# One transformer-like layer on one core: the branch projection's operands taken in groups, and the last product of the down projection added in banks that are already open

## The chip, the cores and the metric

The kernel runs on one core of a Trainium2 chip as a single launch. The metric is the device time of that launch in microseconds. A core has a matrix engine (TensorE, PE in the profile, with PEld for its weight loads), a vector engine (VectorE, DVE), a scalar engine (ScalarE, ACT), a general engine (GpSimd, POOL), a queue of DMA instructions on SyncE (SP, or SPq), the SBUF that all of them work in, and the PSUM, eight banks of 128 x 512 float32, in which TensorE adds its products up. Engines run at the same time, each through its own instructions in their order, and wait for one another on semaphores.

## What is computed

One layer on x, 1024 positions by 1024 columns. The lines of the reference that matter here:

```python
gates = jax.nn.sigmoid(zg.reshape(B_, S, N_BRANCH, D_MODEL) + b_gate)
merged = (gates[:, :, 0] * (ya @ w_branch[0])      # A: chunked attention
          + gates[:, :, 1] * (yb @ w_branch[1])    # B: forgetting attention
          + gates[:, :, 2] * (yc @ w_branch[2]))   # C: indexed sparse attention
return merged @ w_out
...
x = x + g1 * _rmsnorm(y, norm_g[l, 1])
h = _rmsnorm(x, norm_g[l, 2]) * (1.0 + sc2) + sh2
a, g = jnp.split(h @ w_up, 2, axis=-1)
y = (jax.nn.gelu(conv(a)) * g) @ w_down
x = x + g2 * _rmsnorm(y, norm_g[l, 3])
```

Each of ya, yb, yc is 1024 x 256, each w_branch 256 x 1024, w_down 2816 x 1024. The result must be close to float32, so a product of two matrices is taken as three: each operand is split into a high part (rounded to the engine's fast type) and a low part (what is left), and high x high, high x low and low x high are added.

## The kernel before

**Splitting.** `split` (L226 to L232 of the profile) makes the high part with one ACT copy (L231) and the low part with one DVE subtraction (L232).

**The attention heads and the branch stage.** The twelve heads are written by a hand-made order that mixes their score, transpose and value products with other work of TensorE, among it the gates (`g`, L247 to L249). The last head is the fourth of branch C: ACT and DVE make the high and low parts `C3ph` (L838) and `C3pl` (L839) of its transposed probabilities, and PE takes the products `C3y` (L822, L823). Where it is not ordered by hand, a scheduler places each engine's instructions. After the heads comes the branch stage: for each branch b (0 to 2) the two pieces `yb` of y are loaded from DRAM and split into `y_0h`, `y_0l`, `y_1h`, `y_1l`; then for each of eight column tiles m, the tile's weights (`wbr`, 128 x 2 x 128, 128 KB) are loaded (L1002), cast by ACT (L1003) and subtracted by DVE (L1004) into `wb`; the gate tile `tgb` comes back from DRAM (L1007; four gates of branch 2 are computed here instead); twelve matmuls `yp` (L1017 to L1019) fill two banks out of a ring of three; and DVE multiplies each bank by gate + 1 (L1021; into `M` for branch 0, into `tgb` after it). For branches 1 and 2 POOL adds that to `M` (L1023). `yb` and `tgb` share a ring of seven tiles (`k4`), `wbr` one of three.

**The down projection and the end.** The last part multiplies in rounds n = 0 to 6 with seven products per 2 x 2 block (a Strassen-like plan), each round into four banks; a table says which, and to which part of `acc` they are added. Round 4 uses the banks `V`, rounds 5 and 6 the banks `X`; `down_add` (L1643) adds a bank to `acc` on DVE. One inner slice of w_down is left over and taken as a plain product: its left operands are loaded from `F_spill` (into `ring`, L1513), its right ones are `wl`. `final_block` takes, for one block `tb` of 128 positions, that product in two halves of 512 columns (L1612 to L1614, six matmuls each, into banks of their own), and for each half: DVE adds the bank to `acc` (L1615), ACT squares it with a sum (L1616), POOL or DVE multiplies by the gain (L1617). Then DVE adds the two sums (L1619), DVE and POOL make the reciprocal root (L222, L224), DVE multiplies and adds the residual in two halves (L1623), and each half is stored. Even blocks go after round 4, odd blocks after round 6.

Of the kernel before, what the change touches and what calls it, by code (L numbers as in the profile page):

```python
# [27 lines left out]
N_RAW, N_E, N_K4, N_B4, N_STK, N_PT, N_BI, N_P4 = 3, 5, 7, 7, 4, 2, 1, 12  # L28
# [16 lines left out]
YG_POOL = (2, 2, 2, 2, 2, 2, 2, 1)  # L45
# [15 lines left out]
def encoder_layer(ctx: ExitStack, tc: tile.TileContext, x, w_ada, w_in, w_branch, w_out, w_up, w_down,  # L61
# [929 lines left out]

    M = [None] * KD
    for b in range(3):
        y_s = []
        for j in range(2):
            yt = k4(f"yb{b}_{j}")
            nc.sync.dma_start(yt, y_spill[b, j])
            y_s.append(split(yt, (P, S), f"y{b}_{j}", alloc=lambda n, sh: e4(n, sh, F32R)))
# [600 lines left out]
    def final_block(tb, banks):  # L1599
        xr = (e4 if tb % 3 else raw4)(f"xf{tb}")  # L1600
        nc.sync.dma_start(xr, x1_spill[tb * P:(tb + 1) * P, :])
        ss2 = sm(f"n3_{tb}ss2", 2)
        i, odd = tb // 2, tb % 2
        y, yg = acc[:, tb], work[:, 4 + i]
        sq = small.tile([P, HALF], F32, tag="ada_acc", name=f"sq{tb}", bufs=1)
        for e in range(2):
            o = banks[e]
# [1 line left out]
            for k in range(2):
                l, r = fin[k][0][odd], fin[k][1][e]  # L1610
                lh, ll = (l[:, j, i * P:(i + 1) * P] for j in range(2))
                pe.matmul(o, lh, r[:, 0], start=(k == 0), stop=False)  # L1612
                pe.matmul(o, lh, r[:, 1], start=False, stop=False)
                pe.matmul(o, ll, r[:, 0], start=False, stop=(k == 1))  # L1614
# [157 lines left out]
```

## Time and profile before

| | us |
|---|---|
| runs of the kernel before | 1581.08, 1584.87, 1584.56; median 1584.56 |
| the profiled execution | 1577.21 |
| its span in the trace | 1575.4 |
| PE busy | 1493.3 (95%) |
| DVE busy | 1157.1 (73%) |
| ACT busy | 787.0 (50%) |
| POOL busy | 559.6 (36%) |
| chain that ended last | PE 69%, DVE 15%, DMA 5%, issue 4%, ACT 4%, SPq 2%, POOL 1% |

The span is measured from the first instruction to the last in the trace; 1.8 us of the execution lie outside it. Busy shares are means over a span with very different stages, so they say which engine is full, and not where it waits: that is read from the timeline of PE, stretch by stretch. A bracket behind a row of a timeline is the time that the engine sat idle before that row, and the instruction that ended it.

### The profile page before, as it was taken

To read this page: it belongs to the slowest core of one execution; us is meant where nothing else is said; L and a number is where in the kernel's file an instruction comes from. 1 tells how busy PE (TensorE), PEld (TensorE's weight loads), DVE (VectorE), ACT (ScalarE), POOL (GpSimd) and SP (SyncE) were. 2 spreads that over 40 slices of the span, in tenths; PEclk is the share of its full clock that TensorE was granted. 3 is DMA by queue.
4 is the path that set the end of the run, shared out by engine and by line. 5 is a ranking of instruction groups with operands and counts; after the bars stand their busy time and mean duration, and the time that the engine had idled before them with its cause. 6 is when DMAs were issued, how large, how long until landed. Compare 5 with 4: busy or idle time off the path is not lost.

```text
span 1575.4 us, 21143 instructions
## 1 busy us (share of the span) xinstructions
PE 1493.3 (95%) x7322; PEld 1234.4 (78%) x7322; DVE 1157.1 (73%) x2106; ACT 787.0 (50%) x1462; POOL 559.6 (36%) x396
## 2 busy tenths in 40 slices
PE   3989999999998999998999989999999999999996
PEld 2878888887887788776888778788888887788885
DVE  6665888998559755557536779888778777879868
ACT  4434698886554444532235455555555554522222
POOL 3632544343443443205542323222223222323305
PEclk9999999999999999999999999999999999999999
DMA  9541332344443452346666412444444445898762
GB/s 287 137 107 47 105 111 84 124 129 131 122 132 90 121 160 88 111 150 204 217 265 215 142 54 94 170 158 166 152 146 164 153 148 173 329 354 293 280 227 108
DMA packets 181727, 253.98 MB, mean 161 GB/s; under 512 B 14891, under 2 KB 132851, under 8 KB 181619
## 3 DMA queue, kind: packets, MB, share of 16 engines
q1 hardware_dynamic: 181619, 252.62, 48.3%
q8 instruction: 58, 0.95, 0.3%
q14 instruction: 50, 0.41, 0.1%
HBM read 169.75 MB, written 74.97 MB: 155 GB/s over the span
## 4 chain that ended last, share of the span: by engine, by line
PE 69%; DVE 15%; DMA 5%; issue 4%; ACT 4%; SPq 2%; POOL 1%; DVEq 0%; POOLq 0%; ACTq 0%
PE g L247 4%; PE g L248 4%; PE X L1268 4%; PE g L249 4%; PE X L1269 4%; PE X L1270 4%; PE X L1632 2%; PE X L1633 2%; PE X L1634 2%; PE V L1268 2%; PE V L1269 2%; PE V L1270 2%; PE V L1632 2%; PE V L1633 2%; PE V L1634 2%
## 5 line engine op out<-in xcount | busy, mean ns | idle before, releaser
L669 ACT ACTIVATE junk<-sc,thr 128x512 bf16<-128x512 f32 (+2 forms) x93 | 80.1, 861 | 25.6 <-DVE thr L690 19.7
L671 DVE TENSOR_SCALAR_CACHE_REDUCE junk<-sc,thr 128x384 bf16<-128x384 f32 (+2 forms) x93 | 89.8, 966 | 1.9
L1234 POOL TENSOR_TENSOR T<-ua 128x512 f32<-128x512 f32 x21 | 27.2, 1294 | 175.7 <-DVE rT L1220 166.1
L1312 POOL TENSOR_TENSOR cv<-cv,g 128x1024 f32<-128x1024 f32 x22 | 57.1, 2598 | 49.3 <-ACT cv L1311 35.4
L1269 PE MATMUL X<-left_S,rT 128*128 128x512 f32 (+1 forms) x184 | 70.8, 385 | 0.2 <-DVE left_S L1114 0.2
L1268 PE MATMUL X<-left_S,rT 128*128 128x512 f32 (+1 forms) x184 | 70.8, 385 | 0.0
L1270 PE MATMUL X<-left_S,rT 128*128 128x512 f32 (+1 forms) x184 | 70.7, 384 | 0.0
L1522 ACT ACTIVATE T<-work 128x512 fp32r<-128x512 f32 x40 | 25.0, 631 | 63.2 <-PE V L1634 26.1
L1235 POOL TENSOR_TENSOR ug<-ug 128x512 f32<-128x512 f32 x22 | 33.0, 1501 | 65.2 <-DVE ua L1228 65.2
L1643 DVE TENSOR_TENSOR acc<-acc,X 128x512 f32<-128x512 f32 x68 | 45.7, 683 | 13.6 <-PE X L1634 13.3
L1023 POOL TENSOR_TENSOR M<-M,tgb 128x1024 f32<-128x1024 f32 x12 | 30.6, 2567 | 66.0 <-DVE tgb L1021 62.2
L585 DVE SCALAR_TENSOR_TENSOR ada_acc<-ada_row,c_act,ada_acc 128x512 f32<-128x512 f32 x42 | 39.3, 936 | 12.9 <-DMA ada_row<-in_w_ada 12.4
L1633 PE MATMUL X<-T,ring 128*128 128x512 f32 x120 | 47.0, 392 | 0.0
L1634 PE MATMUL X<-T,ring 128*128 128x512 f32 x120 | 46.7, 390 | 0.0
L1632 PE MATMUL X<-T,ring 128*128 128x512 f32 x120 | 46.2, 393 | 0.0
L1643 DVE TENSOR_TENSOR acc<-acc,V 128x512 f32<-128x512 f32 x56 | 37.3, 682 | 11.6 <-PE V L1634 11.1
L1220 DVE TENSOR_TENSOR rT<-ua,rT 128x512 fp32r<-128x512 f32 x45 | 38.7, 861 | 9.3 <-ACT rT L1219 9.0
L1219 ACT ACTIVATE rT<-ua 128x512 fp32r<-128x512 f32 x45 | 28.2, 627 | 33.0 <-DVE ua L1232 22.6
L1220 DVE TENSOR_TENSOR rB<-ua,rB 128x512 fp32r<-128x512 f32 x44 | 40.8, 931 | 2.0 <-ACT rB L1219 0.9
L1269 PEld LDWEIGHTS X<-left_S,rT 128*128 128x128 f32 x184 | 34.5, 187 | 8.0 <-DVE left_S L1114 0.4
L1270 PEld LDWEIGHTS X<-left_S,rT 128*128 128x128 f32 x184 | 34.5, 187 | 7.7
L637 DVE SCALAR_TENSOR_TENSOR sc<-rl,wi,sc 128x512 f32<-128x512 f32 (+3 forms) x30 | 30.2, 1038 | 14.0 <-ACT rl L636 14.0
(988 smaller groups left out, 5559.8 us busy)
## 6 DMA issues: line engine op xcount, KB each, us to landing
ring<-L_spill SPq DMA_DIRECT2D x70, 512.0 KB, 6.0
L_spill<-S SPq DMA_DIRECT2D x40, 512.0 KB, 4.0
L_spill<-A SPq DMA_DIRECT2D x30, 512.0 KB, 3.1
raw_g<-in_w_in SPq DMA_DIRECT2D x24, 512.0 KB, 4.1
ada_row<-in_w_ada SPq DMA_DIRECT2D x24, 512.0 KB, 4.0
ua<-in_w_up SPq DMA_DIRECT2D x22, 512.0 KB, 4.3
ug<-in_w_up SPq DMA_DIRECT2D x22, 512.0 KB, 3.9
gate_spill<-tg SPq DMA_DIRECT2D x20, 512.0 KB, 2.7
```

The costliest lines, as they stand in the source:

```text
L247: pe.matmul(o, wh[:, k], hh[:, k, ts_], start=(k == 0), stop=False)
L248: pe.matmul(o, wh[:, k], hl[:, k, ts_], start=False, stop=False)
L669: act.activation(junk_a[:, 0:n], scores[b], AF.Sign, scale=-1.0, bias=t_f, accum_out=cnt[:, j:j + 1])
L671: dve.tensor_scalar(junk_d[:, 0:n], scores[b], t_f, None, op0=OP.is_lt, op1=OP.add, accum_out=cnt[:, j:j + 1])
L1220: eng.tensor_tensor(hl_[1], src, hl_[0].bitcast(F32), op=OP.subtract)
L1268: pe.matmul(oc, r[:, 0, k], lh, start=(first and k == 0), stop=False, skip_group_check=True)
L1269: pe.matmul(oc, r[:, 0, k], ll, start=False, stop=False, skip_group_check=True)
L1270: pe.matmul(oc, r[:, 1, k], lh, start=False, stop=(last and k == 3), skip_group_check=True)
L1632: pe.matmul(o, lh, r[:, 0], start=(starts and k == 0), stop=False, skip_group_check=True)
L1633: pe.matmul(o, lh, r[:, 1], start=False, stop=False, skip_group_check=True)
L1634: pe.matmul(o, ll, r[:, 0], start=False, stop=(k == 1), skip_group_check=True)
L1643: dve.tensor_tensor(dst, dst, banks[i], op=OP.add)
```

## The change

Two places are changed.

**The branch stage.** The weights come in six loads of 512 KB, four column tiles each (`branch_w`), are split by `split` (one ACT copy, one DVE subtraction of 128 x 1024), and group g + 1 is asked for when tile 1 of group g is reached. The pieces of y are loaded and split by `branch_y`: those of branch 0 ahead of the stage, those of branch b + 1 loaded at tile 2 of branch b and split at tiles 4 and 6. The tiles of the low parts and the weights lie in other pools (the four slots `w4` of the gates' weights, thirteen slots `p4` where there were twelve).

**The end.** `final_block` becomes a class `Final` with four steps. In the last chunk, the half of the plain product that belongs to round 4's part of `acc` (columns 512 to 1023 of the even blocks) is added by PE in the bank `V` that still holds round 4's product, so one DVE addition takes both; so is the half that belongs to round 6's part (columns 0 to 511 of the odd blocks) in the bank `X`. The other halves have a bank of their own, as before. Eight DVE additions are gone (28 to 20 from round 4 on). The odd blocks are taken one by one within round 6, with ACT, DVE and POOL in written order.

```diff
-N_RAW, N_E, N_K4, N_B4, N_STK, N_PT, N_BI, N_P4 = 3, 5, 7, 7, 4, 2, 1, 12
+N_RAW, N_E, N_K4, N_B4, N_STK, N_PT, N_BI, N_P4 = 3, 5, 7, 7, 4, 2, 1, 13
...
+    def branch_y(b):
+        raws = []
+        for j in range(2):
+            raws.append(k4(f"yb{b}_{j}"))
+            nc.sync.dma_start(raws[j], y_spill[b, j])
+        n_y = iter(range(4))
+        def place(n, sh):
+            i = next(n_y)
+            return p4r(n, sh) if b == 1 and i else e4(n, sh, F32R)
+        def steps():
+            for j in range(2):
+                y_next.append(split(raws[j], (P, S), f"y{b}_{j}", alloc=place))
+                yield
+        return steps()
+    def branch_w(g):
+        rb = raw4(f"wbr{g}", (P, 2, HALF))
+        nc.sync.dma_start(rb, w_branch[g // 2][:, g % 2 * HALF:(g % 2 + 1) * HALF].rearrange("(k p) c -> p k c", p=P))
+        return split(rb, (P, 2, HALF), f"wb{g}", alloc=w4 if g < 4 else p4r)
...
     for b in range(3):
-        y_s = []
-        for j in range(2):
-            yt = k4(f"yb{b}_{j}")
-            nc.sync.dma_start(yt, y_spill[b, j])
-            y_s.append(split(yt, (P, S), f"y{b}_{j}", alloc=lambda n, sh: e4(n, sh, F32R)))
+        y_s, y_next = y_next, []
         for m in range(KD):
-            wb = p4r(f"wb{b}_{m}", (P, 2, 2, P))
-            rb = raw4(f"wbr{b}_{m}", (P, 2, P))
-            nc.sync.dma_start(rb, w_branch[b][:, m * P:(m + 1) * P].rearrange("(k p) c -> p k c", p=P))
-            act.activation(wb[:, 0], rb, AF.Copy)
-            dve.tensor_tensor(wb[:, 1], rb, wb[:, 0].bitcast(F32), op=OP.subtract)
+            if m % 4 == 0:
+                wb = wb_next
+            elif m % 4 == 1 and (b < 2 or m < 4):
+                wb_next = branch_w(b * 2 + m // 4 + 1)
+            if b < 2:
+                if m == 2:
+                    y_steps = branch_y(b + 1)
+                elif m in (4, 6):
+                    next(y_steps)
...
+                if c == N_C - 1 and n == 4:
+                    final_operands()
+                    evens = [Final(2 * i) for i in range(4)]
+                elif c == N_C - 1 and n == 6:
+                    odds = [Final(2 * i + 1) for i in range(4)]
+                    loads.enter_context(tc.manual_schedule(engines={E.Activation, E.DVE, E.Pool}))
                 for i, _ in enumerate(down_mm(n, next_ops())):
-                    down_add(n, i)
+                    if c < N_C - 1 or n not in (4, 6):
+                        down_add(n, i)
+                    elif n == 4:
+                        evens[i].half(1, VB[i], False)
+                        evens[i].gained(1)
+                    else:
+                        odds[i].half(0, XB[i], False)
+                        if i:
+                            odds[i - 1].norm()
+                        odds[i].gained(0)
+                        odds[i].half(1, VB[i], True)
+                        if i == 3:
+                            odds[3].gained(1)
+                            odds[3].norm()
+                        if i:
+                            odds[i - 1].end()
+                        if i < 3:
+                            odds[i].gained(1)
```

In the order of each engine, nothing is moved outside these two places. PE has the same matmuls in both kernels; DVE has 26 instructions fewer, ACT ten, SP eighteen.

On ACT, in head C3 (`C3e` are exponentials of its scores, `tg_4` a gate, `C3ph` the high parts that PE waits for), the kernel before has:

```order
L794 ACTIVATE C3e_6823,C3rs_6857<-C3e_6823,C3m_6838 128x640
L838 ACTIVATE C3ph_0_6873<-C3t_0_6868 128x512
L794 ACTIVATE C3e_6840,C3rs_6859<-C3e_6840,C3m_6855 128x768
L530 ACTIVATE tg_4_6768<-g_4_1_6782,gate_b 128x512
L838 ACTIVATE C3ph_1_6890<-C3t_1_6886 128x384
L846 ACTIVATE y_6004<-C3y_6867 64x256
L231 ACTIVATE y_0h<-yb_0_7091 128x1024
```

and the changed one:

```order
L793 ACTIVATE C3e_6823,C3rs_6857<-C3e_6823,C3m_6838 128x640
L837 ACTIVATE C3ph_0_6873<-C3t_0_6868 128x512
L793 ACTIVATE C3e_6840,C3rs_6859<-C3e_6840,C3m_6855 128x768
L230 ACTIVATE wb0h<-wbr_7103 128x1024
L529 ACTIVATE tg_4_6768<-g_4_1_6782,gate_b 128x512
L837 ACTIVATE C3ph_1_6890<-C3t_1_6886 128x384
L845 ACTIVATE y_6004<-C3y_6867 64x256
L230 ACTIVATE y_0h<-yb_0_7091 128x1024
```

The copy of the first weight group stands ahead of a gate and of `C3ph_1`. On DVE, the subtraction `wb0l` stands in the same way ahead of `C3pl_1`.

On PE, at the end of the last head (`C3t` transposes, `C3y` value products), the kernel before has:

```order
L833 MATMUL C3t_3_7063<-ident,C3e_6924 128x128 x2
L822 MATMUL C3y_7010<-C3ph_2_7047,Cv 128x256
L823 MATMUL C3y_7010<-C3pl_2_7048,Cv 64x256
L822 MATMUL C3y_7010<-C3ph_2_7047,Cv 128x256
L823 MATMUL C3y_7010<-C3pl_2_7048,Cv 64x256
L822 MATMUL C3y_7010<-C3ph_3_7067,Cv 128x256
L823 MATMUL C3y_7010<-C3pl_3_7068,Cv 64x256
L822 MATMUL C3y_7010<-C3ph_3_7067,Cv 128x128
L823 MATMUL C3y_7010<-C3pl_3_7068,Cv 64x128
L1017 MATMUL yp_0_0_7111<-y_0h,wb_0_7103 128x512
L1018 MATMUL yp_0_0_7111<-y_0l,wb_0_7103 128x512
```

and the changed one:

```order
L821 MATMUL C3y_7010<-C3ph_2_7047,Cv 128x256
L822 MATMUL C3y_7010<-C3pl_2_7048,Cv 64x256
L821 MATMUL C3y_7010<-C3ph_2_7047,Cv 128x256
L822 MATMUL C3y_7010<-C3pl_2_7048,Cv 64x256
L1046 MATMUL yp_0_0_7112<-y_1l,wb0h 128x512
L1047 MATMUL yp_0_0_7112<-y_1h,wb0l 128x512
L1046 MATMUL yp_0_1_7120<-y_1l,wb0h 128x512
L1047 MATMUL yp_0_1_7120<-y_1h,wb0l 128x512
L821 MATMUL C3y_7010<-C3ph_3_7067,Cv 128x256
L1046 MATMUL yp_1_0_7137<-y_1l,wb0h 128x512
L1047 MATMUL yp_1_0_7137<-y_1h,wb0l 128x512
L822 MATMUL C3y_7010<-C3pl_3_7068,Cv 64x256
```

Eighteen `yp` matmuls (twelve of them further up, between the transposes and `C3y_2`) stand among the head's own products, where all of them came behind it. Further on, on DVE, the subtraction of the first y piece of branch 2 stands ahead of branch 1's first multiplication, and those of weight group 3 and of the second piece behind that one and the next.

On DVE at the end (`acc` additions, `n_5ss` to `n_7` the steps to a block's factor, `xf` the last multiplication and addition), the kernel before ends with:

```order
L1615 TENSOR_TENSOR acc<-acc,X_12167 128x512
L1617 TENSOR_TENSOR work<-acc,G_1_12173 128x512
L1623 SCALAR_TENSOR_TENSOR xf_13912<-work,n_3r,xf_13912 128x512 x2
L1619 TENSOR_TENSOR n_7ss<-n_7ss_13978 128x1
L1623 SCALAR_TENSOR_TENSOR xf_13944<-work,n_5r,xf_13944 128x512 x2
L222 TENSOR_SCALAR n_7_14000<-n_7ss 128x1
L1623 SCALAR_TENSOR_TENSOR xf_13976<-work,n_7r,xf_13976 128x512 x2
```

and the changed one with:

```order
L1647 TENSOR_TENSOR acc<-acc,V_12086 128x512
L1665 SCALAR_TENSOR_TENSOR xf_13771<-work,n_3r,xf_13771 128x512 x2
L1647 TENSOR_TENSOR acc<-acc,X_12083 128x512
L1658 TENSOR_TENSOR n_5ss<-n_5ss_13776 128x1
L221 TENSOR_SCALAR n_5_13897<-n_5ss 128x1
L1647 TENSOR_TENSOR acc<-acc,V_12087 128x512
L1654 TENSOR_TENSOR work<-acc,G_1_12089 128x512
L1658 TENSOR_TENSOR n_7ss<-n_7ss_13779 128x1
L221 TENSOR_SCALAR n_7_13914<-n_7ss 128x1
L1665 SCALAR_TENSOR_TENSOR xf_13774<-work,n_5r,xf_13774 128x512 x2
L1665 SCALAR_TENSOR_TENSOR xf_13777<-work,n_7r,xf_13777 128x512 x2
```

Each odd block's last step now stands right behind the next block's second addition, where three blocks' last steps stood in a row at the end.

## Rows read from the trace of the kernel before

**Rows 1.** Stretches: from:to, length, busy us (count) by engine, granted clock, DMA share, GB/s

```profile
720.00:740.00 20.00, 17.10 (x74) 13.38 (x73) 14.08 (x18) 3.55 (x8) 13.21 (x6) 1.00 0.73 233
...
760.00:780.00 20.00, 20.00 (x90) 16.50 (x89) 9.36 (x11) 5.79 (x9) 8.58 (x4) 1.00 0.72 258
...
691.00:695.00 4.00, 3.91 (x10) 3.08 (x11) 1.25 (x3) 1.14 (x4) 0.00 (x0) 0.57 0.74 267
```

**Rows 2.** Timeline of PE, head C3: start, duration, operation, idle before and releaser

```profile
670.41 0.33 PE L823 MATMUL C3y<-C3pl,Cv 128*64 128x256 f32 x1 [0.20 <-DVE C3pl L839]
...
681.40 0.38 PE L822 MATMUL C3y<-C3ph,Cv 128*128 128x256 f32 x1 [0.41 <-ACT C3ph L838]
681.99 0.33 PE L823 MATMUL C3y<-C3pl,Cv 128*64 128x256 f32 x1 [0.21 <-DVE C3pl L839]
...
690.13 0.33 PE L823 MATMUL C3y<-C3pl,Cv 128*64 128x256 f32 x1 [0.66 <-DVE C3pl L839]
...
691.09 0.51 PE L1017 MATMUL yp<-y_0h,wb 128*128 128x512 f32 x1 [0.51 <-ACT wb L1003]
```

**Rows 3.** Timeline of PE, branch stage: its rows with idle time, one neighbour

```profile
703.55 0.40 PE L1019 MATMUL yp<-y_1h,wb 128*128 128x512 f32 x1
705.30 0.51 PE L1017 MATMUL yp<-y_0h,wb 128*128 128x512 f32 x1 [1.36 <-ACT wb L1003]
...
718.72 0.73 PE L1017 MATMUL yp<-y_1h,wb 128*128 128x512 f32 x2 [0.74 <-ACT y_1h L231]
723.59 0.50 PE L1017 MATMUL yp<-y_0h,wb 128*128 128x512 f32 x1 [1.83 <-DVE tgb L1021]
738.67 0.50 PE L1017 MATMUL yp<-y_0h,wb 128*128 128x512 f32 x1 [1.07 <-DVE tgb L1021]
745.20 0.50 PE L1017 MATMUL yp<-y_0h,wb 128*128 128x512 f32 x1 [0.65 <-DVE tgb L1021]
```

**Rows 4.** Waits from 680 to 757: us in total, times, longest

```profile
ACT y_0h L231 <- DMA yb<-y_spill: 12.1, 2, 7.8
ACT wb L1003 <- DMA wbr<-in_w_branch: 11.7, 5, 3.6
```

**Rows 5.** Timeline of ACT, head C3: a copy of 128 x 1024

```profile
671.30 1.06 ACT L231 ACTIVATE y_0h<-yb 128x1024 fp32r<-128x1024 f32 x1
```

**Rows 6.** Timeline of DVE, head C3 and start of branch 1: three subtractions

```profile
679.80 1.22 DVE L232 TENSOR_TENSOR y_0l<-yb,y_0h 128x1024 fp32r<-128x1024 f32 x1
...
722.51 0.43 DVE L1004 TENSOR_TENSOR wb<-wbr,wb 128x256 fp32r<-128x256 f32 x1 [2.58 <-ACT wb L1003]
...
724.64 2.32 DVE L1004 TENSOR_TENSOR wb<-wbr,wb 128x256 fp32r<-128x256 f32 x1
```

**Rows 7.** Tile tgb: shortest, median and longest time of its loads

```profile
DMA to landing us min/median/max: 3.4/4.5/7.8
```

**Rows 8.** Timeline of POOL at the end: root of block 2, two gain products

```profile
1542.95 0.55 POOL L224 TENSOR_TENSOR n_2r<-n,mhalf 128x1 f32<-128x1 f32 x1
1543.47 3.00 POOL L1617 TENSOR_TENSOR work<-acc,G 128x512 f32<-128x512 f32 x2
```

**Rows 9.** Timeline of DVE at the end: block 2's last step, an addition, the last row

```profile
1543.53 3.48 DVE L1623 SCALAR_TENSOR_TENSOR xf<-work,n_2r,xf 128x512 f32<-128x512 f32 x2 [0.16 <-POOL n_2r L224]
...
1547.00 0.67 DVE L1615 TENSOR_TENSOR acc<-acc,V 128x512 f32<-128x512 f32 x1
...
1570.81 1.41 DVE L1623 SCALAR_TENSOR_TENSOR xf<-work,n_7r,xf 128x512 f32<-128x512 f32 x2 [0.66 <-POOL n_7r L224]
```

**Rows 10.** Timeline of PE at the end: first plain product, last matmul

```profile
1531.58 0.39 PE L1612 MATMUL V<-wl,ring 128*128 128x512 f32 x1
...
1563.17 0.40 PE L1614 MATMUL X<-wl,ring 128*128 128x512 f32 x1
```

**Rows 11.** Timeline of SP: stretch in which the four F_spill loads are issued

```profile
1514.90 7.81 SPq L1513 DMA_DIRECT2D ring<-F_spill  x4
```

**Rows 12.** Tile ring from 1512 on: shortest, median and longest time of its loads

```profile
DMA to landing us min/median/max: 3.5/5.9/6.6
```

More of the change, by code (lines that the diff above doesn't have):

```diff
@@ L44 @@
 L_AHEAD = 4
-YG_POOL = (2, 2, 2, 2, 2, 2, 2, 1)
 N_BANKS = {"d": 2, "s": 3, "n": 3}
@@ L1597, in final_operands @@
                                                None if j else w4) for e in range(2)]))
[L1599 to L1607, printed above, removed]
-            es = slice(e * HALF, (e + 1) * HALF)
[L1609 to L1614, printed above, removed]
-            dve.tensor_tensor(y[:, es], y[:, es], o, op=OP.add)
-            act.activation(sq, y[:, es], AF.Square, accum_out=ss2[:, e:e + 1])
-            (pool if e < YG_POOL[tb] else dve).tensor_tensor(yg[:, es], y[:, es], G2[e], op=OP.mult)
-        ss = sm(f"n3_{tb}ss")
-        dve.tensor_tensor(ss, ss2[:, 0:1], ss2[:, 1:2], op=OP.add)
-        r = rstd_of(ss, f"n3_{tb}")
-        for e in range(2):
-            es = slice(e * HALF, (e + 1) * HALF)
-            dve.scalar_tensor_tensor(xr[:, es], yg[:, es], r, xr[:, es], op0=OP.mult, op1=OP.add)
-            nc.sync.dma_start(out[tb * P:(tb + 1) * P, es], xr[:, es])
@@ new lines, in encoder_layer, with __init__, half, gained @@
+    class Final:
+        def __init__(self, tb):
+            self.tb, self.i, self.odd = tb, tb // 2, tb % 2
+            self.xr = (e4 if tb % 3 else raw4)(f"xf{tb}")
+            nc.sync.dma_start(self.xr, x1_spill[tb * P:(tb + 1) * P, :])
+            self.ss2 = sm(f"n3_{tb}ss2", 2)
+            self.y, self.yg = acc[:, tb], work[:, 4 + self.i]
+        def half(self, e, o, start):
+            for k in range(2):
+                l, r = fin[k][0][self.odd], fin[k][1][e]
+                lh, ll = (l[:, j, self.i * P:(self.i + 1) * P] for j in range(2))
+                pe.matmul(o, lh, r[:, 0], start=(start and k == 0), stop=False, skip_group_check=True)
+                pe.matmul(o, lh, r[:, 1], start=False, stop=False, skip_group_check=True)
+                pe.matmul(o, ll, r[:, 0], start=False, stop=(k == 1), skip_group_check=True)
+            es = slice(e * HALF, (e + 1) * HALF)
+            y = self.y[:, es]
+            dve.tensor_tensor(y, y, o, op=OP.add)
+            sq = small.tile([P, HALF], F32, tag="ada_acc", name=f"sq{self.tb}", bufs=1)
+            act.activation(sq, y, AF.Square, accum_out=self.ss2[:, e:e + 1])
+        def gained(self, e):
+            es = slice(e * HALF, (e + 1) * HALF)
+            y = self.y[:, es]
+            (dve if e and self.tb == NB - 1 else pool).tensor_tensor(self.yg[:, es], y, G2[e], op=OP.mult)
+        def norm(self):
+            ss = sm(f"n3_{self.tb}ss")
+            dve.tensor_tensor(ss, self.ss2[:, 0:1], self.ss2[:, 1:2], op=OP.add)
+            self.r = rstd_of(ss, f"n3_{self.tb}")
+        def end(self, halves=(0, 1)):
+            tb, xr, r = self.tb, self.xr, self.r
+            for e in halves:
+                es = slice(e * HALF, (e + 1) * HALF)
+                dve.scalar_tensor_tensor(xr[:, es], self.yg[:, es], r, xr[:, es], op0=OP.mult, op1=OP.add)
+                nc.sync.dma_start(out[tb * P:(tb + 1) * P, es], xr[:, es])
```

28 lines of the change are left out of this document (17 added, 11 removed).

## The prediction

> **What bounds the kernel now.** The first view is the busy time by stretch [rows 1]. From 760 on PE is busy all the time (20.00 us of 20, 90 matmuls, so 0.22 us from one to the next); a change elsewhere can't shorten that. From 720 to 740 it is busy 17.10 us, and no other engine is full, so there something is waited for. Between 691 and 695 the granted clock is 0.57: most of that stretch ran at the lower of the clock's two levels (1.2 GHz), right behind the gaps at the end of head C3.
>
> The second view is the timeline of PE in those stretches, of which the rows with an idle bracket count. At the end of head C3 four stand from 681.40 on [rows 2]: 0.41, 0.21, 0.66 and 0.51 us, three ended by C3's own high and low parts, the last by the first weight cast. In the branch stage there are five [rows 3]: 1.36, 0.74, 1.83, 1.07, 0.65, sum 5.65. An idle gap costs more than its bracket: from 703.55 to 705.30 are 1.75 us where 0.23 is usual, that is 0.16 over the 1.36 of the bracket, and the matmul behind it lasts 0.51 instead of 0.40. So I add 0.28 for each gap.
>
> The third view says who was late. ACT waited 12.1 us for the two loads of y and 11.7 us in five waits for weights [rows 4]; since it works in order, the cast that PE needs stood behind them. Later PE waits for DVE's multiplication, which stands behind a weight subtraction: 0.43 us alone, 2.32 us for the same size once POOL adds to M [rows 6].
>
> At the end, PE is through at 1563.17 + 0.40 = 1563.57 and DVE at 1570.81 + 1.41 = 1572.22 [rows 9, 10]: 8.65 us in which the matrix engine does nothing.
>
> **The change part by part.**
>
> (1) End of head C3. Eighteen yp matmuls are put between the head's products. That is 18 x 0.22 = 4.0 us of work where the four gaps are, 1.79 us, with 0.28 each 2.9 us. Cover is lost for the last pieces only: weight group 1's subtraction (1.22 us, as long as the first row of [rows 6]) now stands ahead of the last C3pl on DVE, and the next yp waits for a bank that is emptied behind that. Two of the eighteen stand in this place, so I leave 0.5 us of stall. Gain 2.4 us, bounds 1 and 2.9.
>
> (2) The clock. 691 to 695 at 0.57 is 4.0 x 0.43 = 1.7 us lost. The low level came after PE had idled at 690 and 691 [rows 2]; with those gaps filled I expect full clock. Gain 1.7, bounds 0 (the same happens at another gap) and 1.7.
>
> (3) The first weight group in head C3. Its copy (1.06 us, [rows 5]) stands ahead of C3ph_1 on ACT, its subtraction (1.22 us) ahead of C3pl_1 on DVE. There PE already waited 0.20 us for C3pl_1 at 670.41 [rows 2], so there is no slack: C3pl_1 comes some 1.06 to 1.3 us later, and PE, whose next scores stand behind C3y, with it. I take a loss of 1.3; bounds 0.8 (part of it is made up by the scores' own waits behind it) and 2.5 (copy and subtraction one after the other, and the gap's 0.28).
>
> (4) The branch stage. The casts are ahead by four tiles and y by a branch, so the waits of [rows 4] need no longer end a gap of PE: the five gaps, 5.65 + 5 x 0.28 = 7.1 us, can go. 18 casts and 18 subtractions fewer cost nothing where they were and aren't on the path. What is late next: at the start of branch 1, DVE holds the subtraction of branch 2's first y piece ahead of the first multiplication, then weight group 3, then the second piece, three of 1.22 us. The load behind the first is issued on SP after a gate tile that waits until branch 1's own second piece is split, at tile 6 of branch 0; some six loads of 512 KB are then in flight at once, and such loads landed after 3.4 to 7.8 us, median 4.5 [rows 7]. Three banks give PE two groups of six matmuls, 2.7 us, before it waits for the first multiplication. With the median I get the multiplication late by 0.4 to 3 us beyond that and take 1.2; for weight group 5, whose subtraction meets POOL at work as in the last row of [rows 6], 0.5. So 7.1 - 1.7 = 5.4, bounds 2 and 7.1.
>
> (5) The F_spill loads are needed earlier: the first plain product was at 1531.58 [rows 10] and now stands 23 matmuls, 5.1 us, sooner, at about 1526.5. The four loads are issued from 1514.90 on within 7.81 us [rows 11] and landed after at most 6.6 us [rows 12], so the first pair is there at about 1522, and the third load, needed some 13 matmuls later, by 1529.3 at the worst. No cost; if that cover fails, PE waits one for one.
>
> (6) The end. Eight DVE additions of 0.67 us [rows 9] go, 5.4 us of work. Are they on the path? An odd block's last step takes 1.41 us alone and 3.48 us, in the last and the first row of [rows 9], when POOL has its two gain products (3.00 us, started 0.06 us earlier, [rows 8]): the two engines take turns. In the changed order each odd block has just this pattern, POOL's root (0.55), then its two gains against DVE's two halves (3.48), one further addition (0.67) and the small steps (about 0.3): 5.0 us for each block, while PE needs 18 x 0.22 = 4.0 us. So DVE and POOL set the pace, the removed additions shorten what DVE had waited for, and the last block's steps end about when they did. I take a gain of 0.3; bounds -1.3 (one more gain product of POOL in the last chain) and 5.4 (all of the additions). Of the two ends I stay near the lower one, because the row of 3.48 is the same pattern.
>
> The Trainium skill has a rule on that place, in "SBUF — State Buffer", section "Who interferes with whom": a DVE instruction with two SBUF inputs contends with a GpSimd instruction that reads SBUF, the one that issues first goes on and the other blocks, and one with at most one SBUF input doesn't contend. By that rule the additions from PSUM are the very DVE work that POOL doesn't hold up, so taking them out frees nothing of the held chain; the trace agrees (3.48 us against 1.41). By a count of DVE's instructions alone the sum would be 5.1 us better.
>
> **Sum.** 2.4 + 1.7 - 1.3 + 5.4 + 0.3 = 8.5 us. The profiled execution took 1577.21 us and would take 1568.7, its span 1566.9 instead of 1575.4. The median of the three runs shown is 1584.56, 7.35 us over the profiled one; taking the gain from it gives **1576.1 us**.
>
> **The rivals.**
>
> (a) The end gives all its additions back: DVE isn't held by POOL in the new order, and the tail after the last matmul shrinks from 8.65 to about 3.5 us. For it: the tail is long, and the odd blocks are spread out. Against: the 3.48 us. 1576.1 - 5.1 = 1571.0.
>
> (b) The branch stage's gaps come back as late gate tiles and y pieces: these share seven tiles, y now holds two of them for most of a branch, and a landing of 7.8 us instead of 4.5 delays every multiplication. For it: the last three gaps of [rows 3] are ended by the multiplication, not by a cast, and the DMA share there is 0.73 already [rows 1]. Then (4) brings nothing: 1576.1 + 5.4 = 1581.5.
>
> (c) The change doesn't do what it says at the end of C3: weight group 1 is copied into a slot of a gate's weights and so waits on ACT for the last of that gate's matmuls, with the head's last C3ph behind it; yp then fills no gap, and the clock still falls. (1) and (2) are lost: 1576.1 + 4.1 = 1580.2.
>
> (d) Slower: late 512 KB loads stop PE so long that the clock falls each time, as at 691. One such place costs 7.8 - 4.5 = 3.3 us of wait, 0.28, and 1.7 of clock, 5.3 us. The places are the start and middle of branch 1 and the start of branch 2, with (3) as a fourth that adds 1.7. All: 15.9 + 1.7 - 1.7 (the stalls that the sum already holds) = 15.9, so 1576.1 + 15.9 = 1592.0. From two places on the kernel is slower than before. Against it: DMA stands at 0.73, and the clock stayed at 1.00 through the gaps of 720 to 740 [rows 1].
>
> **How the numbers follow.** Forecast 0.55, (a) 0.13, (b) 0.17, (c) 0.10, (d) 0.05. The forecast's own range, with the bounds of (1) to (6), is 1572.5 to 1580. The range from 1570.5 to 1582 takes in (a), (b) and (c) and leaves (d) and the far ends out. A measurement of this kernel tells a difference from none at about 0.3%, 4.75 us: faster is below 1579.8, slower above 1589.3. Faster: nearly all of the forecast (0.53), (a) (0.13), a third of (c) and a fifth of (b) (0.07): 0.73. Slower: 0.04, from (d). Within: 0.23.
>
> **What would show it.** Right: no idle bracket on PE between 681 and 692, granted clock 1.00 there, one gap near 670 of about 1.3 us, at most 1.7 us of gaps between 692 and 745, and still over 8 us from the last matmul to DVE's last row, with pairs of 3.5 us in DVE's last multiplications. Wrong: gaps ended by a gate tile's load or by ACT's copies in branch 1 (b, d), a row of C3 ended by ACT behind the copy of weight group 1 (c), or a tail of 4 us (a).

## The result and the profile after

| | median, us | runs, us | ratio to before |
|---|---|---|---|
| before | 1583.85 | 1581.08 to 1584.87 (4) | |
| changed | 1573.33 | 1570.51 to 1576.28 (4) | 0.9938, 95% interval 0.9920 to 0.9956 |

In all that follows two runs are left out that fell in a slow state, one of 7479.96 us of the kernel before and one of 2919.52 us of `gain_one_half`.

The change makes the kernel faster, by 7 to 13 us on the interval. The profiled execution of the changed kernel took 1573.15 us, its span 1571.3. The two spans differ by only 4.1 us, because the profiled execution of before was a quick one: its projection banks `pm`, in code that both kernels share, begin at 78.91 us, and at 82.53 to 83.74 in the changed kernel and in all nine experiments. So the gain is read from one mark to another inside the trace, not from span to span. Three marks on PE serve for the whole study: the last row of the matmuls `ada_ps` in the heads, which comes ahead of both edits' effects, the 19th `yp` matmul, by which all of head C3 and the same eighteen `yp` matmuls are done in either order, and the first matmul `row` behind the branch stage. Timeline of PE, before (start, duration, engine, line, operation; in brackets the idle time before it and what ended it):

```profile
635.66 0.50 PE L588 MATMUL ada_ps<-one,ada_acc 128*128 128x1 f32 x4
...
696.91 0.39 PE L1018 MATMUL yp<-y_1l,wb 128*128 128x512 f32 x1
...
809.70 0.49 PE L1043 MATMUL row<-ident,mod 128*128 128x128 f32 x3
```

And of the changed kernel, with every row between the first and the last mark that has an idle bracket from 668 on:

```profile
639.07 0.51 PE L587 MATMUL ada_ps<-one,ada_acc 128*128 128x1 f32 x4
...
674.18 0.39 PE L821 MATMUL C3y<-C3ph,Cv 128*128 128x256 f32 x1 [0.67 <-ACT C3ph L837]
675.10 0.34 PE L822 MATMUL C3y<-C3pl,Cv 128*64 128x256 f32 x1 [0.53 <-DVE C3pl L838]
...
696.26 0.50 PE L1046 MATMUL yp<-y_1l,wb0h 128*128 128x512 f32 x1 [0.68 <-DVE y_1l L231]
...
699.10 0.50 PE L1045 MATMUL yp<-y_0h,wb0h 128*128 128x512 f32 x1 [0.78 <-DVE M L1049]
...
804.51 0.60 PE L1071 MATMUL row<-ident,mod 128*128 128x128 f32 x4
```

From the first mark to the last: 174.04 us before, 165.44 after, 8.6 us less. The gaps of [rows 2] and [rows 3] are gone, and four others stand in head C3. The row of 699.10 is the 19th `yp`: up to there it was 61.25 us before and 60.03 after, from there on 112.79 and 105.41. So 1.2 us of the gain lie ahead of that mark and 7.4 behind it. The windows (busy us and count of PE, PEld, DVE, ACT, POOL; granted clock, DMA share, GB/s) answer to [rows 1]:

```profile
691.00:695.00 4.00, 4.00 (x28) 3.60 (x27) 1.40 (x3) 2.07 (x3) 0.00 (x0) 1.00 0.00 0
...
700.00:720.00 20.00, 20.00 (x90) 16.51 (x89) 15.51 (x22) 5.92 (x6) 0.00 (x0) 1.00 0.97 348
720.00:740.00 20.00, 20.00 (x89) 16.37 (x88) 10.86 (x15) 1.06 (x1) 18.21 (x8) 1.00 0.62 201
```

PE is full from 700 on, with 90 and 89 matmuls in 20 us, where 74 stood from 720 to 740 in [rows 1]. The DMA share is 0.97 from 700 to 720, and no gap comes of it. ACT still waits long there, 12.7 us for a slot of weight group 5 and 7.7 for y, and in this execution PE is not late for that:

```profile
ACT wb5h L230 <- PE yp L1046: 12.7, 1, 12.7
...
ACT y_0h L230 <- DMA yb<-y_spill: 7.7, 1, 7.7
```

The y of that second wait is covered by little: its copy on ACT starts at 716.72 and takes 1.06 us, and DVE's subtraction of it, which stands ahead of branch 1's first multiplication, starts at 718.11, 0.33 us after the copy's end. Experiment 3 shows an execution in which that cover fails.

At the end the changed kernel has the pattern of the first row of [rows 9] twice. Timeline of DVE, of the odd blocks 1 and 3 and of the last, 7:

```profile
1551.33 0.69 DVE L1647 TENSOR_TENSOR acc<-acc,X 128x512 f32<-128x512 f32 x1 [0.75 <-PE X L1644]
1551.93 0.76 DVE L1658 TENSOR_TENSOR n_1ss<-n_1ss 128x1 f32<-128x1 f32 x1
...
1553.55 3.49 DVE L1665 SCALAR_TENSOR_TENSOR xf<-work,n_1r,xf 128x512 f32<-128x512 f32 x2
...
1557.55 0.14 DVE L1658 TENSOR_TENSOR n_3ss<-n_3ss 128x1 f32<-128x1 f32 x1
...
1558.55 3.44 DVE L1665 SCALAR_TENSOR_TENSOR xf<-work,n_3r,xf 128x512 f32<-128x512 f32 x2
...
1566.77 1.41 DVE L1665 SCALAR_TENSOR_TENSOR xf<-work,n_7r,xf 128x512 f32<-128x512 f32 x2
```

and of POOL and PE in the same place:

```profile
1550.13 2.55 POOL L1654 TENSOR_TENSOR work<-acc,G 128x512 f32<-128x512 f32 x2 [2.19 <-DVE acc L1647]
...
1553.48 3.01 POOL L1654 TENSOR_TENSOR work<-acc,G 128x512 f32<-128x512 f32 x2
...
1559.37 0.40 PE L1644 MATMUL V<-wl,ring 128*128 128x512 f32 x1
```

PE is through at 1559.77 and DVE at 1568.18: a tail of 8.41 us where [rows 9, 10] gave 8.65. From the mark `row` to the end of the last matmul are 753.87 us before and 755.26 after, 1.39 more. The other traces have 754.54 to 757.41 there, and the longest is `end_alone`, which has the stage of before; `branch_alone`, with the end of before, has 755.30. So I take this for a difference between executions; what makes it stays open.

### The profile page after: what moved, and what is told of

Its sections match the earlier page's. It is cut to its first block, busy times and chain, and to the rows that moved or that the text cites. A ratio compares the mean times of both kernels' runs of the same rounds, so it can differ in the third digit from the quotient of the medians.

```text
span 1571.3 us, 21017 instructions
## 1 busy us (share of the span) xinstructions
PE 1488.9 (95%) x7322; PEld 1231.8 (78%) x7322; DVE 1144.9 (73%) x2080; ACT 783.3 (50%) x1444; POOL 557.3 (35%) x396
## 4 chain that ended last, share of the span: by engine, by line
PE 69%; DVE 17%; DMA 4%; issue 4%; ACT 3%; SPq 2%; POOL 1%; DVEq 0%; ACTq 0%; POOLq 0%
PE X L1296 4%; PE X L1297 4%; PE X L1298 4%; PE g L246 4%; PE g L247 4%; PE g L248 4%; PE X L1674 2%; PE X L1675 2%; PE X L1676 2%; PE V L1296 2%; PE V L1297 2%; PE V L1298 2%; PE V L1674 2%; PE V L1675 2%; PE V L1676 2%
## 5 line engine op out<-in xcount | busy, mean ns | idle before, releaser
L584 DVE SCALAR_TENSOR_TENSOR ada_acc<-ada_row,c_act,ada_acc 128x512 f32<-128x512 f32 x42 | 39.3, 937 | 12.7 <-DMA ada_row<-in_w_ada 12.3
```

## The experiments

The theory (A): the stage brings nearly all, by gaps of PE that go; the end brings nothing, because DVE and POOL take turns there. The rivals are in the expectations: that the two edits share the gain, that one half of the stage's edit does it alone, that the end is held by something else.

**1. Each edit alone.** `branch_alone` is the changed kernel with the old `final_block`, `end_alone` the kernel before with the new end:

```diff
# branch_alone, against the changed kernel
-                    elif n == 4:
-                        evens[i].half(1, VB[i], False)
...
+                    for i in range(4):
+                        final_block(2 * i, VB[i % 2 * 2:i % 2 * 2 + 2])
...
```

> Only the branch stage is changed (weights in groups of four column tiles, y one branch ahead), the end is that of the kernel before. Theory A (the stage brings nearly all, the end's additions were off the path): about 8.6 us faster than before, ratio 0.9946, no idle bracket on PE in branches 1 and 2, tail from the last matmul to the last row of DVE 8.6 us as before. Rival B (both parts matter, the end brings 4 to 5 us that one profile hides): 4 to 5 us faster, ratio 0.997.

> Only the end is changed (the last plain product is added in the open banks, odd blocks one by one), the branch stage is that of the kernel before. Theory A: 0.2 to 0.3 us faster, ratio 1.000 within its interval, tail 8.4 us, pairs of 3.5 us in DVE's last multiplications of the odd blocks. Rival B: 4 to 5 us faster, ratio 0.997, tail about 4 us.

| | median, us | ratio to before | interval |
|---|---|---|---|
| branch_alone | 1572.51 | 0.9944 | 0.9928 to 0.9959 |
| end_alone | 1582.68 | 1.0002 | 0.9991 to 1.0014 |

The stage alone is the whole gain, as far as these runs can tell (8.9 us, 6.5 to 11.4, against the 9.8 of both edits), and the end alone moves nothing that they can tell. From mark to mark `branch_alone` takes 165.74 us. `end_alone` has the stage of before, in a second execution, and it shows which of the gaps of [rows 2, 3] are fixed and which are chance. Timeline of PE, `end_alone`:

```profile
686.10 0.39 PE L822 MATMUL C3y<-C3ph,Cv 128*128 128x256 f32 x1 [0.41 <-ACT C3ph L838]
686.69 0.33 PE L823 MATMUL C3y<-C3pl,Cv 128*64 128x256 f32 x1 [0.21 <-DVE C3pl L839]
...
694.83 0.33 PE L823 MATMUL C3y<-C3pl,Cv 128*64 128x256 f32 x1 [0.66 <-DVE C3pl L839]
...
695.79 0.50 PE L1017 MATMUL yp<-y_0h,wb 128*128 128x512 f32 x1 [0.51 <-ACT wb L1003]
...
710.70 0.50 PE L1017 MATMUL yp<-y_0h,wb 128*128 128x512 f32 x1 [3.65 <-ACT wb L1003]
```

The four gaps of C3 [rows 2] come back to the hundredth (0.41, 0.21, 0.66, 0.51). The clock behind them doesn't. A window of `end_alone`, which answers to 692 to 694 of before (its first `yp` starts at 695.79, that of before at 691.09):

```profile
696.00:698.00 2.00, 2.00 (x10) 1.62 (x10) 0.68 (x3) 0.86 (x3) 0.00 (x0) 1.00 0.72 250
```

and of before:

```profile
692.00:694.00 2.00, 2.00 (x6) 1.51 (x6) 0.00 (x0) 0.19 (x1) 0.00 (x0) 0.50 0.78 281
```

Ten matmuls in 2 us at full clock against six at 0.50. So the 1.7 us of half clock were lost in the one profile of before and not in the other execution of the same code. In `end_alone` the cast of the first gap of [rows 3] came later: ACT stood 8.57 us for the load of y ahead of it, and PE idled 3.65 us where before had 1.36.

**2. y ahead alone, weights in groups alone.** In `y_ahead` the weights come tile by tile as before; in `w_groups` y is loaded at the start of its own branch as before. Both keep the new end.

```diff
# y_ahead
-            if m % 4 == 0:
-                wb = wb_next
-            elif m % 4 == 1 and (b < 2 or m < 4):
-                wb_next = branch_w(b * 2 + m // 4 + 1)
+            wb = p4r(f"wb{b}_{m}", (P, 2, 2, P))
+            rb = raw4(f"wbr{b}_{m}", (P, 2, P))
...
+            act.activation(wb[:, 0], rb, AF.Copy)
+            dve.tensor_tensor(wb[:, 1], rb, wb[:, 0].bitcast(F32), op=OP.subtract)
...
# w_groups
-        y_s, y_next = y_next, []
+        y_s = []
+        for j in range(2):
+            yt = k4(f"yb{b}_{j}")
+            nc.sync.dma_start(yt, y_spill[b, j])
+            y_s.append(split(yt, (P, S), f"y{b}_{j}", alloc=lambda n, sh: e4(n, sh, F32R)))
...
```

> The changed kernel, except that the weights of the branch stage come tile by tile as before (128 KB, a cast and a subtraction for each tile); y is loaded and split one branch ahead. No yp matmul then stands among head C3's products. Theory A (the gaps of the branch stage have two causes, late weights and late y, and the end of C3 needs the weight groups): the gaps ended by y's copy go, those ended by weight casts and by multiplications behind weight subtractions partly stay; the end of C3 keeps its four gaps and its half clock. From the last ada_ps matmul to the first row matmul 169 to 171 us (before 173.8, after 165.2), ratio to before about 0.998. Theory B (ACT standing behind y's loads was the cause of all five gaps): 166.5 us, ratio 0.9955.

> The changed kernel, except that y is loaded and split at the start of its own branch as before; the weights come in groups of four tiles, one group ahead. The 18 yp matmuls stand among head C3's products as in the changed kernel. Theory A (y must be ahead as well): the end of C3 is as in the changed kernel, but at the starts of branches 1 and 2 PE stands 2 to 5 us for y's load, copy and subtraction, and the clock may fall: from the last ada_ps matmul to the first row matmul 170 to 175 us, ratio 0.997 to 1.001. Theory C (the groups alone bring it): 166 us, ratio 0.995.

All times from the first mark, in us (the expectations count from the last of the four `ada_ps` matmuls, 0.25 us later than the start of their row):

| | 19th yp | row | between | ratio to before |
|---|---|---|---|---|
| before | 61.25 | 174.04 | 112.79 | |
| end_alone (stage of before) | 59.64 | 173.69 | 114.05 | 1.0002 |
| changed | 60.03 | 165.44 | 105.41 | 0.9938 |
| branch_alone | 60.03 | 165.74 | 105.71 | 0.9944 |
| y_ahead | 59.66 | 167.89 | 108.23 | 0.9973, 0.9960 to 0.9985 |
| w_groups | 60.03 | 167.67 | 107.64 | 0.9957, 0.9943 to 0.9971 |

Neither theory of the expectations holds in full. I had given `y_ahead` 169 to 171 us or 166.5, and `w_groups` 170 to 175 or 166; both lie between. By the marks each half by itself takes about 6.1 to 6.4 us from the stage, and the two together 8.6: they remove the same waits to a large part. The times of the runs are too coarse for that: by their ratios `y_ahead` gains 4.3 us (2.4 to 6.3), `w_groups` 6.8 (4.6 to 9.0) and both 9.8 (7.0 to 12.7). Four gaps are left in `y_ahead` behind C3, none over 0.42 us, two ended by weights and two by multiplications; three of them are

```profile
705.93 0.50 PE L1046 MATMUL yp<-y_0h,wb 128*128 128x512 f32 x1 [0.42 <-DVE wb L1026]
...
717.62 0.50 PE L1046 MATMUL yp<-y_0h,wb 128*128 128x512 f32 x1 [0.41 <-DVE wb L1026]
...
743.20 0.47 PE L1044 MATMUL yp<-y_0h,wb 128*128 128x512 f32 x1 [0.28 <-DVE tgb L1048]
```

and `w_groups` has one behind its 19th `yp`:

```profile
723.97 0.50 PE L1044 MATMUL yp<-y_0h,wb2h 128*128 128x512 f32 x1 [1.22 <-DVE tgb L1048]
```

ACT's waits fit that. The waits of `y_ahead` from 680 to 757 (us in total, times, longest) have

```profile
ACT wb L1025 <- DMA wbr<-in_w_branch: 18.6, 6, 4.5
```

and those of `w_groups`

```profile
ACT y_0h L230 <- DMA yb<-y_spill: 4.4, 2, 2.8
```

In `y_ahead` ACT stood longer for weights than before (18.6 us against the 11.7 of [rows 4]), but for a load of y only 0.4 us, once, and PE lost little by it: a late cast no longer had a second late load in front of it. In `w_groups` ACT stood 4.4 us for y where before had 12.1. That the two waits covered each other in this way is how I read these rows; the runs themselves show only that the gains overlap.

The second column says what the eighteen `yp` matmuls between C3's products are worth. `y_ahead` has none of them there and all four old gaps, at full clock, and no weight group in head C3; it is 0.37 us sooner at the 19th `yp` than the changed kernel. A window of it, with the gaps of 0.66 and 0.51 us (ended at 692.35 and 693.31):

```profile
692.00:694.00 2.00, 1.14 (x6) 0.90 (x7) 0.98 (x3) 1.31 (x4) 0.00 (x0) 1.00 0.95 297
694.00:696.00 2.00, 2.00 (x11) 1.62 (x10) 0.69 (x2) 0.41 (x2) 0.00 (x0) 1.00 0.79 278
```

So that part of the change, the filling and the first weight group together, fills gaps and makes others of the same size.

**3. The waits at the end of C3.** On the changed kernel's DVE, the rows ahead of its last two gaps:

```profile
694.99 1.22 DVE L231 TENSOR_TENSOR y_1l<-yb,y_1h 128x1024 fp32r<-128x1024 f32 x1 [0.70 <-PE C3t L832]
...
698.35 1.88 DVE L1049 SCALAR_TENSOR_TENSOR M<-tgb,yp 128x512 f32<-128x512 f32 x3 [0.54 <-PE C3y L822]
```

DVE wrote `y_1l` only when PE's last transposes `C3t` were done, which read the tile that had been in its slot, and the first `M` only behind C3's last product `C3y`. Behind these stand the 0.68 and the 0.78 us. That the slots are the cause is read from what ended DVE's idle time and from the pools of the kernel. `y1l_slot` gives `y_1l` another slot, and `wb0_on_pool` moves the first group's subtraction from DVE to POOL, against the gap of 0.53 at 675.10:

```diff
# y1l_slot
-            return p4r(n, sh) if b == 1 and i else e4(n, sh, F32R)
+            return p4r(n, sh) if (b == 1 and i) or (b == 0 and i == 3) else e4(n, sh, F32R)
# wb0_on_pool
-        return split(rb, (P, 2, HALF), f"wb{g}", alloc=w4 if g < 4 else p4r)
+        return split(rb, (P, 2, HALF), f"wb{g}", eng=None if g else pool, alloc=w4 if g < 4 else p4r)
```

> The changed kernel, with the low part of branch 0's second y piece (y_1l) in a slot of the pool p4 that is free early, where it had taken a slot that holds C3's exponentials until the last transposes have read them. The scheduler then also takes the last six of the eighteen yp matmuls out from among C3's last products. Theory A (the stalls of 0.68 and 0.78 us are caused by the slots, and the work that is put between C3's products is worth what it fills): the gap ended by y_1l goes, two gaps of C3ph_3 and C3pl_3 of 0.4 to 0.7 us come back for want of filling; the 19th yp matmul starts 59 to 60 us after the last ada_ps matmul, as in the changed kernel (59.8), the stage takes 165 us. Theory B (the slot alone costs 1 us): 58.8 and 164.2 us.

> The changed kernel with one subtraction moved, that of the first weight group (wb0l), from DVE to POOL; every other engine keeps its order. Theory A (C3ph_1 is late by ACT's copy alone, 0.67 us, and C3pl_1 by DVE's subtraction on top, 0.53 us): the second gap near 675 falls to about 0.2 us and the first stays, stage 164.5 instead of 165.2 us, ratio 0.9935 where the changed kernel had 0.9938. Rival: POOL's normalisation of C3e stands behind the subtraction there, the scores' transposes come later by 1 to 3 us and the stage takes 166 to 168 us, ratio 0.995.

| | 19th yp | row | ratio to before | interval |
|---|---|---|---|---|
| y1l_slot | 63.33 | 170.45 | 0.9973 | 0.9960 to 0.9985 |
| wb0_on_pool | 59.71 | 165.93 | 0.9939 | 0.9926 to 0.9953 |

`y1l_slot` went 5 us the other way, and both theories were wrong. Timeline of PE:

```profile
695.20 0.38 PE L821 MATMUL C3y<-C3ph,Cv 128*128 128x256 f32 x1 [1.56 <-ACT C3ph L837]
695.80 0.45 PE L822 MATMUL C3y<-C3pl,Cv 128*64 128x256 f32 x1 [0.21 <-DVE C3pl L838]
...
697.78 0.80 PE L1046 MATMUL yp<-y_1l,wb0h 128*128 128x512 f32 x1 [1.32 <-DVE y_1l L231]
```

and of DVE, the subtraction that the last of them waited for:

```profile
696.50 1.22 DVE L231 TENSOR_TENSOR y_1l<-yb,y_1h 128x1024 fp32r<-128x1024 f32 x1 [0.76 <-DMA gate_spill<-tg]
```

The new slot came free even later, when a gate had been written out. So what `y_1l` waited for went with its slot, which shows that the slot makes that wait; what a slot that is free in time would gain, and whether the same holds for `M`, no run here shows. ACT took a y piece of the next branch ahead of the last `C3ph` as well. Behind the 1.56 and 0.21 us of idle time the clock fell, ahead of the 1.32, and it stayed low longer than in before. Windows of `y1l_slot`:

```profile
694.00:696.00 2.00, 0.59 (x2) 0.39 (x3) 1.07 (x2) 1.15 (x2) 0.00 (x0) 0.96 0.68 258
696.00:698.00 2.00, 0.68 (x4) 0.49 (x4) 1.47 (x2) 0.38 (x1) 0.00 (x0) 0.50 0.79 257
...
700.00:702.00 2.00, 2.00 (x6) 1.53 (x5) 1.26 (x2) 0.00 (x0) 0.00 (x0) 0.50 0.96 336
```

In `wb0_on_pool` the second gap near 675 shrank as theory A had it and the first stayed:

```profile
675.67 0.38 PE L821 MATMUL C3y<-C3ph,Cv 128*128 128x256 f32 x1 [0.66 <-ACT C3ph L837]
676.26 0.33 PE L822 MATMUL C3y<-C3pl,Cv 128*64 128x256 f32 x1 [0.21 <-DVE C3pl L838]
```

The 0.32 us gained up to the 19th `yp` are lost again between that and `row` (106.22 us against 105.41). The time is that of the changed kernel within what can be told, and the stage misses theory A's 164.5 us. The 0.8 us are lost in one place, the start of branch 1, from 722 to 727. Timeline of ACT and of DVE there:

```profile
719.29 1.06 ACT L230 ACTIVATE y_0h<-yb 128x1024 fp32r<-128x1024 f32 x1 [9.08 <-DMA yb<-y_spill]
...
720.38 1.23 DVE L231 TENSOR_TENSOR y_0l<-yb,y_0h 128x1024 fp32r<-128x1024 f32 x1 [0.97 <-ACT y_0h L230]
```

The loads of that y landed after 7.1 to 8.3 us, where the changed kernel's landed after 5.7 to 7.0. ACT waited 9.08 us instead of 7.74, DVE's subtraction came 0.97 us late with the first multiplications of branch 1 behind it, and PE waited for those in pieces too short for a bracket (the two largest, 0.24 us each, stand before its matmuls of 723.99 and 725.73). `branch_alone`, which has the changed kernel's stage, loses 0.3 us there (ACT 8.59 us, DVE 0.48).

**4. The end.** Three variants of the changed kernel's odd blocks 1, 3 and 5. `gain_on_dve` takes both gains from POOL and does them on DVE in the last step; `gain_one_half` does so for half 1 alone (the same lines, with `and e` in both conditions); `no_gain_odd` leaves the product with the gain out for these three blocks, so its time is that of less work.

```diff
# gain_on_dve
         def gained(self, e):
+            if self.odd and self.tb < NB - 1:
+                return
...
+                if self.odd and tb < NB - 1:
+                    yg = self.yg[:, es]
+                    dve.scalar_tensor_tensor(yg, self.y[:, es], r, G2[e], op0=OP.mult, op1=OP.mult)
+                    dve.tensor_tensor(xr[:, es], yg, xr[:, es], op=OP.add)
...
```

> The changed kernel, but for odd blocks 1, 3 and 5 POOL makes no gain products: DVE multiplies by factor and gain in one operation and adds the residual in a second, so DVE has six operations of 0.67 us more and POOL six of 1.3 us fewer. Theory A (the taking of turns between DVE and POOL sets the pace, 5.0 us for a block): a block takes DVE 2 x 0.63 + 4 x 0.67 + 0.3 = 4.2 us, no operation of 3.5 us is left, the tail falls from 8.4 to about 5.7 us, 2.7 us faster than the changed kernel, ratio to before 0.992. Rival C (the number of DVE's operations sets the pace): 4 us more work on DVE, tail 8.4 to 12 us, ratio to before 0.994 to 0.997.

> The changed kernel, odd blocks 1, 3 and 5: the gain of half 0 stays on POOL, that of half 1 is taken by DVE inside the last step (two operations in place of one). Theory A (DVE and POOL take turns whenever POOL has a gain product, so one product costs half of what two cost): DVE's last step of blocks 1 and 3 about 2.9 us instead of 3.5, tail from the last matmul to DVE's last row 7.2 to 7.8 us instead of 8.4, ratio 0.993. Rival (what counts is the number of DVE's operations, so one more in each block outweighs it): tail 8.4 to 9, ratio 0.994.

> The changed kernel without the gain products of blocks 1, 3 and 5: their output lacks the factor of the gain. POOL has six operations fewer, DVE the same. Theory A: DVE needs 1.27 + 1.34 + 0.3 = 2.9 us for a block, less than PE's 4.1, so the tail is what follows the last product alone: an addition, the gain product, the small steps and two pairs of 1.4 us, 4.4 to 5 us, 3.5 to 4 us faster than the changed kernel. Rival C: DVE's count is unchanged, so the tail stays at 8.4 us.

| | tail, us | median, us | ratio to before | interval |
|---|---|---|---|---|
| before | 8.65 | 1583.85 | | |
| changed | 8.41 | 1573.33 | 0.9938 | 0.9920 to 0.9956 |
| gain_one_half | 7.91 | 1571.13 | 0.9933 | 0.9919 to 0.9948 |
| gain_on_dve | 8.04 | 1570.62 | 0.9931 | 0.9917 to 0.9945 |
| no_gain_odd | 4.93 | 1567.78 | 0.9910 | 0.9895 to 0.9924 |

(The tail runs from the end of PE's last matmul to the end of DVE's last row. Each ratio is to runs of before of the same set, whose medians were 1581 to 1584 us, so the ratios are what can be compared.) Of the expectations, `no_gain_odd` came as theory A had it (4.4 to 5 us); `gain_on_dve` missed theory A's 5.7 us and `gain_one_half` its 7.2 to 7.8, both to the long side. Without POOL's products DVE's pair is back at its length alone, and the tail is 3.5 us shorter. Timeline of DVE, `no_gain_odd`:

```profile
1556.49 1.41 DVE L1668 SCALAR_TENSOR_TENSOR xf<-acc,n_3r,xf 128x512 f32<-128x512 f32 x2
```

With one product of POOL beside it, in `gain_one_half`, one instruction takes what two take alone, and the two that follow run at their own speed:

```profile
1558.19 1.76 DVE L1672 SCALAR_TENSOR_TENSOR xf<-work,n_3r,xf 128x512 f32<-128x512 f32 x1
1559.87 0.74 DVE L1669 SCALAR_TENSOR_TENSOR work<-acc,n_3r,G 128x512 f32<-128x512 f32 x1
1560.65 0.69 DVE L1670 TENSOR_TENSOR xf<-work,xf 128x512 f32<-128x512 f32 x1
```

So the last step of a block is 3.4 to 3.5 us with two products on POOL, about 3.2 with one, 2.9 (four instructions of 0.69 to 0.75) with both on DVE, and 1.4 with none at all. What DVE saves by not being held, it pays for by doing the product itself. In `gain_on_dve` a block takes 4.39 us from one addition to the next (1552.37 to 1556.76) where the changed kernel takes 4.95 to 5.63, but block 5's last step, which nothing held in the changed kernel (1.42 us from 1565.44), now takes four instructions as well. That is why the best of these gains 0.4 to 0.5 us of tail and not 3.5. `gain_on_dve` has the lowest ratio of all kernels here that compute the whole layer; its interval and that of the changed kernel overlap, so the step beyond is not measured as a gain.

## Why the prediction was right

The time forecast, 1576.1 us, was 2.8 us over the median and inside the changed kernel's runs by 0.2 us; the range held it, and the chance of 0.73 lay on the right side. The runs give a gain of 10.5 us between the medians and of 9.8 by the ratio, 7.0 to 12.7 on the interval. By the marks the profiles give 8.6 us in the stage and 0.24 at the end, 8.8 in all (without the 1.39 us between them), against a sum of 8.5. The mechanism was right in the main: the gaps of the stage went, and the end brought next to nothing. That the sum comes within 0.3 us is luck in part: two terms inside it, (1) and (4), were off by 1.5 and 2.0 us in opposite directions, and a third, (2), was not the kernel's. Nor does the range of 1572.5 to 1580 follow from the bounds of the terms, which add up to gains from -0.8 to 16.3 us.

- **(1) End of C3: 2.4 predicted, mis-sized.** The filling works, and no gap is left between 676 and 696. But the residual stall of 0.5 us was 0.68 + 0.78 + 2 x 0.28 = 2.0 us, which leaves 0.9. I had seen the weight subtraction ahead of the last C3pl; I had not asked in whose slots the new tiles lie: `y_1l` in the one of C3's exponentials and `M`, by what its wait ended on, in the one of an operand of C3's products. So the new work was tied to the end of the head that it was to cover.
- **(2) The clock: 1.7 predicted.** Against the profile of before it came, 1.00 from 691 to 695. But it is no property of the kernel before: `end_alone` and `y_ahead` idle in the same four places, 0.41, 0.21, 0.66 and 0.51 us, and stay at 1.00. A window of one execution was taken for the kernel's. One of three traces with these gaps lost the 1.7, so what the term is worth on average stays open; the bounds had both ends.
- **(3) First group ahead of C3ph_1: -1.3 predicted, right.** 0.67 + 0.53 + 2 x 0.28 of the two gaps at 674 and 675, less the 0.20 + 0.28 that were there before [rows 2], is 1.3. The split is shown by `wb0_on_pool`: with DVE's subtraction away, 0.53 becomes 0.21, and ACT's copy still costs 0.66.
- **(1) to (3) together** were to bring 2.8 us and brought 1.2 against the profile of before and -0.4 against `end_alone`.
- **(4) The branch stage: 5.4 predicted, 7.4 measured** against the profile of before, 8.6 against `end_alone`. The 7.1 us of gaps went whole, and the 1.7 that I gave back for DVE's three subtractions at the start of branch 1 and for weight group 5 did not come: no idle bracket stands in branches 1 and 2. For the start of branch 1, where I gave back 1.2, that is luck of this execution: DVE had 0.3 us to spare, and the same place cost 0.3 us in `branch_alone` and 0.8 in `wb0_on_pool`, by the late load of y that the prediction names. The 0.5 for weight group 5 came in none of these traces.
- **(5) F_spill: 0, right.** No gap of PE stands at the first plain product.
- **(6) The end: 0.3 predicted, 0.24 measured,** with the pairs of 3.49 and 3.44 us and the cycle of 5.0 us (1553.55 to 1558.55) that the prediction worked out from [rows 8, 9]. (The row of 3.48 us there is of block 2, an even one, and not of an odd block as the prediction has it.) `no_gain_odd` shows the mechanism: with POOL's products gone and the number of DVE's instructions unchanged, the pairs take 1.41 us.

Of the rivals, (a) is out: the tail is 8.41 us, not some 3.5, and `end_alone` is 1.0002. (b) is out at its size: the DMA share did rise, to 0.97, and no gap came of it in the changed kernel; a late y piece cost 0.8 us in `wb0_on_pool`, not 5.4. (c) is out as it was told, though its place was the right one to doubt. ACT's copy of weight group 1 did wait for a gate's matmul, with the last `C3ph` behind it, but for 0.57 us only, and no gap of PE ended on it:

```profile
694.13 1.06 ACT L230 ACTIVATE wb1h<-wbr 128x1024 fp32r<-128x1024 f32 x1 [0.57 <-PE g L247]
```

The yp matmuls do fill the gaps, and yet the sum over that place is near zero. (d) did not occur in the changed kernel; `y1l_slot` shows a relative of it, three gaps and 0.50 of clock from 696 on, at 3.3 us up to the 19th `yp`.

The rule of the Trainium skill that the prediction used ("SBUF — State Buffer", section "Who interferes with whom") is borne out beyond the pairs. The addition of 1551.33, with one input from PSUM, took 0.69 us beside POOL's product, and the addition of two sums right behind it, with two SBUF inputs of 128 x 1, took 0.76 us, to the end of POOL's two products (1552.68), where the same operation took 0.14 at 1557.55.

## What to carry to other kernels

When a wait has two causes in a row on the same engine (ACT stood behind y and then behind weights), curing either one can give most of the gain (here 6.1 and 6.4 us by the marks, of 8.6), and costing them separately counts it twice. Before filling a gap with other work, ask which slots that work's tiles lie in: if they are those of the work being covered, the filler ends with the same wait. And take differences from mark to mark in the trace, with a second execution of the old code beside it: here 3.6 us of the span and 1.6 us of half clock belonged to one execution and not to the kernel. A cover that holds in one trace by 0.3 us is not yet a cover: a second execution shows it.

## What the runs showed of the hardware

- The same four idle stretches on PE were followed by a granted clock of 0.50 in one execution (692 to 694, before) and 1.00 in two others (`end_alone`, `y_ahead`); 1.56 and 0.21 us of idle time were followed by 0.50 in `y1l_slot` (from 696 on, and still from 700 to 702, with a third gap of 1.32 us in between). What decides between them stays open here. The Trainium skill ("TensorE: Matmul & The Clock Gate", section "Part 1: The HAM clock gate") says that the gate's view of activity runs free of the program, so that the same matmuls can meet it differently from one run to the next; these executions agree with that, but none of them shows the cause.
- A DVE instruction of 128 x 1 with two SBUF inputs is held by POOL like a large one: 0.76 us against 0.14, again 0.77 in `end_alone` (1563.64), and 1.06 in the kernel before (1564.03).
- The subtraction of 128 x 1024 that takes DVE 1.22 us took POOL 2.37 (`wb0_on_pool`):

```profile
674.95 2.37 POOL L231 TENSOR_TENSOR wb0l<-wbr,wb0h 128x1024 fp32r<-128x1024 f32 x1
```
